# The value pass of a two-layer decoder: 25 pairs of value chunks by Strassen's scheme

## The chip, the cores and the metric

The kernel runs on one core of a Trainium2 chip. The metric is the device time of one execution in microseconds (us); the kernel before has a median of 1827.03 us over three runs (1826.66 to 1827.59). In the rows of a profile the engines are PE (TensorE, matrix products; PEld is its load of the stationary operand), DVE (VectorE), ACT (ScalarE), POOL (GpSimd) and SP, whose queue issues the loads.

## The reference, cut to what matters

Two layers transform x (256 tokens of 1024 numbers). Each has a token mixer and then a channel mixer in which every token picks 128 of 16384 experts (8 heads of 16) and adds up their value rows:

```python
        u = u_tab[eid]
        act = jax.nn.gelu(jnp.einsum('nhkd,nd->nhk', u, xb).astype(jnp.float32), approximate=False)
        coef = (gw * act).astype(x.dtype)
        return jnp.einsum('nhk,nhkd->nd', coef, v_tab[eid])
...
        x = layer_norm(DN_ALPHA * x + y, ln2_g[i], ln2_b[i])
```

The kernel doesn't gather. It computes `u_tab @ x` for all 16384 experts, multiplies by gates that are zero for experts not picked, and multiplies the resulting 16384 x 256 matrix of coefficients with the whole value table: `y = coef^T @ v_tab`, with 16384 rows of 1024 values read from memory once per layer. That last product is the value pass. Everything is fp32.

## The kernel before

**Three products for one.** The fast fp32 product of the PE keeps fewer bits than fp32. Each operand is therefore split in two: the high part H is the operand cast (on ACT, L100 for values, L236 for coefficients), the low part L is the operand minus H (on DVE, L115 and L237, or partly on POOL). `mm3` (L172) then issues three matmuls into one PSUM bank: H·H, H·L and L·H (L174 to L176). A value of `pool_cols` says how many columns of a low part POOL computes; in the value pass it is 0, so all of it lies on DVE.

**The value pass** (`peer_layer`, L1143 on) runs over 128 chunks of 128 experts. Chunk i has a coefficient tile of 128 experts x 256 tokens (`lo` holds chunks 0 to 63, `hi` the others) and a value tile of 128 experts x 1024 columns. The output is cut into two token tiles `tt` and two halves `k` of 512 columns, four PSUM banks `y[tt][k]` in which all chunks accumulate. A chunk is thus four products of 128 x 128 by 128 x 512, of three matmuls each: 12 matmuls.

**What is issued when.** There is no scheduler: each engine works through its instructions in the order in which the loop emits them, and waits at an instruction whose input or buffer isn't ready. Step i of the loop first calls `next` (L140), which through `pump` (L80) casts and subtracts the values of chunk i+2; then `coef(i + 2)` splits the coefficients of chunk i+2; then come the 12 matmuls of chunk i. There are three buffers of split values (`HL_BUFS`), so the cast of chunk i+2 waits until the PE has finished chunk i-1, whose buffer it takes. The loads come in on SP's queue into five buffers (`RAW_BUFS`), counted by `n_flight`; a chunk's buffer is given back when it has been split, and the next load is issued then.

**The end of the pass.** The last 3 chunks of layer 0 and the last 6 of layer 1 (`kept`) are held back, and their products are issued bank by bank, so that `norm` (L268) can begin on a bank that is complete: it adds it to ALPHA times x on DVE (L286) and goes on to the layer norm. In layer 1 three of the six have buffers of their own (`eH`, `eL`). Layer 0 also loads and splits, between its value chunks, the inputs for the next layer's attention memory: four `memT` parts (subtracted on POOL) and four `wkv` chunks (cast on ACT, subtracted on DVE), at chunks 68, 74, ... 110.

**Banks.** PSUM has eight banks of 512 columns; the pass uses four.

Of the kernel before, what the change touches and what calls it, by code (L numbers as in the profile page):

```python
# [7 lines left out]
F32 = mybir.dt.float32  # L8
F32R = mybir.dt.float32r
# [4 lines left out]
ALU = mybir.AluOpType  # L14
# [4 lines left out]
P = 128  # L19
D = 1024  # L20
T = 256
DT = 8
ALPHA = 4.0 ** 0.25
EPS = 1e-5
GSCALE = 32768.0
N0 = 64
# [21 lines left out]
class Trunk:  # L48
    def __init__(self, ctx, tc, A, out):
        self.ctx, self.tc, self.nc, self.A, self.out = ctx, tc, tc.nc, A, out  # L50
        pool = lambda name, bufs=1, **k: ctx.enter_context(tc.tile_pool(name=name, bufs=bufs, **k))
        self.const = pool("const")
        self.raw = pool("raw", RAW_BUFS)
        self.hl = pool("hl", HL_BUFS)
        self.small = pool("small", 2)
        self.ps = pool("ps", 8, space=PSUM)
        self.items = []
        self.flip = False
        self.sides = []
        self.n_load = self.n_split = self.n_got = self.n_flight = 0  # L60
        self.kept = {}
        self.loaded, self.split = {}, {}

    def bank(self):
# [15 lines left out]
    def pump(self, upto):  # L80
        nc = self.nc
        upto = min(upto, len(self.items))
        while self.n_split < upto:
            i = self.n_split
            self.load(i + 1)
            ap, n, dest, keep, cuts = self.items[i]
            r = self.loaded.pop(i)
            self.n_split += 1
            if keep is not None:
                self.kept[keep] = r  # L90
                continue
            if type(dest) is int:
                h, l = self.extra[dest]
            elif dest is None:
                h = self.hl.tile([P, D], F32R, name="wH")[:, :n]
                l = self.hl.tile([P, D], F32R, name="wL")[:, :n]
            else:
                h, l = dest()
            for c in cuts:
                (nc.vector.tensor_copy if self.cast_dve else nc.scalar.copy)(h[:, c], r[:, c])  # L100
            k = n if getattr(dest, "pool", False) else min(n, self.pool_cols)
            if len(cuts) > 1:
                for c in cuts:
                    e = (nc.vector, nc.gpsimd)[c.start > 0]
                    e.tensor_sub(l[:, c], r[:, c], h[:, c].bitcast(F32))
                k = n
            elif k and self.chained:
                nc.vector.tensor_sub(l[:, k:], r[:, k:], h[:, k:].bitcast(F32))  # L108
                k += 2
                nc.gpsimd.tensor_sub(l[:, :k], r[:, :k], h[:, :k].bitcast(F32))  # L110
                k = n
            elif k:
                nc.gpsimd.tensor_sub(l[:, :k], r[:, :k], h[:, :k].bitcast(F32))  # L113
            if k < n:
                rest = lambda l=l, r=r, h=h, k=k: nc.vector.tensor_sub(l[:, k:], r[:, k:], h[:, k:].bitcast(F32))  # L115
# [151 lines left out]

    def norm(self, y, last, early, fill=False):  # L268
        nc, x = self.nc, self.x
        fine = early or last  # L270
        while "b" not in self.kept:
            self.pump(self.n_split + 1)
        g, b = self.kept["g"], self.kept["b"]
# [4 lines left out]
        Q = 256  # L278

        def add(tt, k):  # L280
            if fine and tt and k:
                q0, n = 1 + k, 1
            else:
                q0, n = 2 * k, 2
            xs = x[:, tt, q0 * Q:(q0 + n) * Q]
            nc.vector.scalar_tensor_tensor(xs, xs, ALPHA, y[tt][k][:, :n * Q], op0=ALU.mult, op1=ALU.add)  # L286
            return tt, q0, n

        def half(tt, q0, n):
# [68 lines left out]
        if fill:  # L358
            yield
            part = add(1, 0)  # L360
# [666 lines left out]
    def peer_layer(self, layer):  # L1027
        nc, tc, A = self.nc, self.tc, self.A
        with ExitStack() as ctx:
# [110 lines left out]
            self.pool_cols, self.chained = 0, False  # L1140
            kept = HL_BUFS + (EXTRA if layer else 0)

            def coef(i):  # L1143
                src = lo[:, i, :] if i < N0 else hi[:, i - N0, :]
# [7 lines left out]
            gl = cp.tile([P, T], F32, name="gl", bufs=1)  # L1152
            nc.scalar.activation(gl, g, AF.Gelu)
            nc.vector.tensor_mul(hi[:, nj - 1, :], hi[:, nj - 1, :], gl)
            y = [[self.bank() for _ in range(2)] for _ in range(2)]
            late = []

            def products(tt, c0, n, part):
                t = slice(tt * P, (tt + 1) * P)
                k, o = divmod(c0, 512)  # L1160
                for i_, (h, l), (cH, cL) in part:
                    self.mm3(y[tt][k][:, o:o + n], cH[:, t], cL[:, t], h[:, c0:c0 + n], l[:, c0:c0 + n],
                             i_ == 0, i_ == P - 1)
            for i in range(P):
                if i + 2 > P - 1:
                    self.pool_cols = 512
                late.append((i, self.next(min(HL_BUFS, P - i)), cs.pop(0)))
                if i + 2 == N0:
# [45 lines left out]
    def plan(self):  # L1214
# [24 lines left out]
        def tail(layer):  # L1239
            for i, dt in enumerate(ORDER[layer]):  # L1240
                self.add(A["w_out"][layer, dt], D, i - 2 if 0 <= i - 2 < EXTRAS[layer] else None)
            norm("ln1", layer)
            for g in range(2):
                for dt in range(DT):
                    self.add(A["w_q"][layer, g, dt], D)
            for i in range(P):
                self.add(A["u"][layer, i], D)
            for i in range(P):
                e = i - P + HL_BUFS + EXTRA
                self.add(A["v"][layer, i], D, e if layer and 0 <= e < EXTRA else None)  # L1250
                k = (i - N0 - 4) // 6
                if layer == 0 and i > N0 and (i - N0 - 4) % 6 == 0 and 0 <= k < 8:
# [110 lines left out]
```

## Time and profile before

| | |
|---|---|
| median of 3 runs | 1827.03 us (1826.66 to 1827.59) |
| the profiled execution | 1825.44 us, its span 1823.7 us |
| PE busy | 1804.1 us, 99% of the span |
| DVE busy | 1307.6 us, 72% |
| ACT busy | 940.7 us, 52% |
| POOL busy | 429.2 us, 24% |
| value pass of layer 0, of layer 1 | 348.17 us from 576.70, 347.92 us from 1467.88 |

The span goes from the first to the last instruction on the core; the time of an execution lies 1.7 us above it. A matmul's record is longer than the time it adds to a stream of matmuls, since they are pipelined: what one adds is read from the starts of its neighbours. The same holds, less strongly, for DVE and ACT.

### The profile page before, as it was taken

The page shows a single profiled execution, that of the slowest core. Times are in us where ns is not written, and L with a number is a line of the kernel's source. Part 1 is how long each engine was busy: PE and PEld are TensorE (multiplying, and loading weights), DVE is VectorE, ACT ScalarE, POOL GpSimd, SP SyncE. Part 2 cuts the span into 40 slices and gives each one's busy share as a digit, 9 for nine tenths or more (in the row PEclk, how much of TensorE's full clock was granted, in tenths as well). Part 3 has the DMA queues.
Part 4 walks back from the last instruction along what each step waited for, and adds up shares of the span by engine and source line. Part 5 has one row for each costly group of instructions (what it writes and reads, how often), then busy time and mean ns, then how long its engine had stood idle before and what let it go on. Part 6 is the DMA issues. An engine that isn't in the chain of part 4 may idle for free.

```text
span 1823.7 us, 33361 instructions
## 1 busy us (share of the span) xinstructions
PE 1804.1 (99%) x12810; PEld 1666.1 (91%) x12810; DVE 1307.6 (72%) x2669; ACT 940.7 (52%) x1614; POOL 429.2 (24%) x324
## 2 busy tenths in 40 slices
PE   8999999999999999999999999999999999999998
PEld 8999999999999888888898899999999988888886
DVE  6684779499998555566668758686999965555556
ACT  6554555455544544555557354554555455444553
POOL 2015762433331000000001368325333300000000
PEclk9999999999999999999999999999999999999999
DMA  7556566655555666667645356666555556666664
GB/s 246 200 160 199 168 202 186 194 167 163 162 162 170 192 194 195 194 214 228 206 171 183 117 176 176 196 196 185 163 163 162 163 181 193 193 195 194 191 194 137
DMA packets 95552, 334.21 MB, mean 183 GB/s; under 512 B 10652, under 2 KB 13728, under 8 KB 95136
## 3 DMA queue, kind: packets, MB, share of 16 engines
q1 hardware_dynamic: 93752, 328.93, 59.2%
q10 hardware_dynamic: 1640, 3.15, 0.5%
q8 instruction: 100, 1.64, 0.4%
q14 instruction: 60, 0.49, 0.1%
HBM read 330.98 MB, written 1.05 MB: 182 GB/s over the span
## 4 chain that ended last, share of the span: by engine, by line
PE 73%; issue 17%; POOL 7%; DVE 2%; ACT 1%; DMA 0%; POOLq 0%; SPq 0%; DVEq 0%; ACTq 0%
PE bank L176 23%; PE bank L174 23%; PE bank L175 23%; POOL wL L110 7%; PE bank L240 2%; ACT wH L100 0%; DVE eL L115 0%; PE bank L333 0%; DVE eH L100 0%; POOL wL L113 0%; PE bank L233 0%; DMA cp<-in_rg_par_dram 0%; DMA raw<-in_w0kg_dram 0%; DVE x L286 0%; DVE wL L115 0%
## 5 line engine op out<-in xcount | busy, mean ns | idle before, releaser
L100 ACT CAST wH<-raw 128x1024 fp32r<-128x1024 f32 (+2 forms) x605 | 626.7, 1037 | 755.3 <-PE bank L176 321.5
L115 DVE TENSOR_TENSOR wL<-raw,wH 128x1024 fp32r<-128x1024 f32 (+3 forms) x413 | 465.6, 1130 | 434.5 <-ACT wH L100 433.9
L174 PE MATMUL bank<-xHL,wH 128*128 128x256 f32 x2536 | 715.2, 282 | 4.8 <-ACT wH L100 4.8
L176 PE MATMUL bank<-xHL,wL 128*128 128x256 f32 x2536 | 702.6, 277 | 0.5 <-DVE wL L115 0.5
L175 PE MATMUL bank<-xHL,wH 128*128 128x256 f32 x2536 | 702.4, 277 | 0.0
L174 PEld LDWEIGHTS bank<-xHL,wH 128*128 128x128 f32 x2536 | 477.4, 188 | 4.8 <-ACT wH L100 4.8
L176 PEld LDWEIGHTS bank<-xHL,wL 128*128 128x128 f32 x2536 | 477.2, 188 | 1.1 <-DVE wL L115 0.7
L175 PEld LDWEIGHTS bank<-xHL,wH 128*128 128x128 f32 x2536 | 477.9, 188 | 0.0
L175 PE MATMUL bank<-wL,cH 128*128 128x512 f32 x1015 | 394.3, 388 | 0.0
L174 PE MATMUL bank<-wH,cH 128*128 128x512 f32 x1015 | 394.3, 388 | 0.0
L176 PE MATMUL bank<-wH,cL 128*128 128x512 f32 x1015 | 394.3, 388 | 0.0
L113 POOL TENSOR_TENSOR wL<-raw,wH 128x1024 fp32r<-128x1024 f32 (+1 forms) x121 | 255.3, 2112 | 210.0 <-ACT wH L100 208.2
L174 PEld LDWEIGHTS bank<-wH,cH 128*128 128x128 f32 x1015 | 190.5, 188 | 39.6
L176 PEld LDWEIGHTS bank<-wH,cL 128*128 128x128 f32 x1015 | 190.5, 188 | 39.3
L175 PEld LDWEIGHTS bank<-wL,cH 128*128 128x128 f32 x1015 | 190.5, 188 | 39.0
L110 POOL TENSOR_TENSOR wL<-raw,wH 128x386 fp32r<-128x386 f32 x126 | 129.5, 1028 | 280.1 <-DVE wL L108 280.1
L322 POOL TENSOR_TENSOR x<-x,raw 128x256 f32<-128x256 f32 x6 | 4.9, 822 | 550.1 <-ACT x L319 550.1
L989 DVE TENSOR_TENSOR oh<-iota,i12T 128x1024 f16<-128x1024 f16 x128 | 130.4, 1019 | 0.0
L108 DVE TENSOR_TENSOR wL<-raw,wH 128x640 fp32r<-128x640 f32 x126 | 104.0, 825 | 7.5
L992 DVE TENSOR_TENSOR oh<-oh,gT 128x1024 f16<-128x1024 f16 x128 | 90.0, 703 | 4.4
L1122 PE MATMUL bank<-oh 128*128 128x128 f16 x1024 | 80.6, 219 | 1.1 <-DVE oh L992 1.1
L1122 PEld LDWEIGHTS <-oh 128*128 128x128 f16 x1024 | 58.6, 97 | 6.0 <-DVE oh L992 1.5
(289 smaller groups left out, 1552.2 us busy)
## 6 DMA issues: line engine op xcount, KB each, us to landing
raw<-in_u_dram SPq DMA_DIRECT2D x256, 512.0 KB, 3.6
raw<-in_v_dram SPq DMA_DIRECT2D x256, 512.0 KB, 4.2
raw<-in_w_q_dram SPq DMA_DIRECT2D x32, 512.0 KB, 4.3
raw<-in_w_out_dram SPq DMA_DIRECT2D x16, 512.0 KB, 4.3
raw<-in_w0qx_dram SPq DMA_DIRECT2D x8, 512.0 KB, 5.1
raw<-in_wkv_dram SPq DMA_DIRECT2D x8, 512.0 KB, 4.6
raw<-in_w0v_dram SPq DMA_DIRECT2D x8, 384.0 KB, 5.7
raw<-in_w0o_dram SPq DMA_DIRECT2D x8, 384.0 KB, 3.2
```

Of the source, the lines that this page charges most:

```text
L100: (nc.vector.tensor_copy if self.cast_dve else nc.scalar.copy)(h[:, c], r[:, c])
L108: nc.vector.tensor_sub(l[:, k:], r[:, k:], h[:, k:].bitcast(F32))
L110: nc.gpsimd.tensor_sub(l[:, :k], r[:, :k], h[:, :k].bitcast(F32))
L113: nc.gpsimd.tensor_sub(l[:, :k], r[:, :k], h[:, :k].bitcast(F32))
L115: rest = lambda l=l, r=r, h=h, k=k: nc.vector.tensor_sub(l[:, k:], r[:, k:], h[:, k:].bitcast(F32))
L174: mm(out, sH, mH, start=start, stop=False, skip_group_check=True)
L175: mm(out, sH, mL, start=False, stop=False, skip_group_check=True)
L176: mm(out, sL, mH, start=False, stop=stop, skip_group_check=True)
L240: self.nc.tensor.matmul(out, lhsT, rhs, start=start, stop=stop, skip_group_check=True)
L989: nc.vector.tensor_tensor(flat(oh[:, 1:3]), self.iota2.unsqueeze(1).to_broadcast([P, 4, P, 2]), pairs(self.i12T[:, j]), op=ALU.is_equal)
L992: nc.vector.tensor_tensor(flat(oh[:, 0:2]), two.rearrange("p z (q e t) -> p z q e t", q=2, t=2), pairs(self.gT[:, j]), op=ALU.mult)
L1122: nc.tensor.matmul(wp[:, qs], oh[:, 2, q // 2, :, q % 2], oh[:, z, q // 2, :, q % 2], start=z == 0, stop=z == 1, skip_group_check=True)
```

## The change

In each layer chunks 8k+2 and 8k+3 form a pair, for k = 1 to 13 (in layer 0 without k = 10): 12 and 13 pairs. Call the pair's coefficient blocks ta, ua (first chunk; tokens 0-127 and 128-255) and tb, ub, and its value halves a0, a1 and b0, b1. Instead of eight products the pair gets seven, by Winograd's form of Strassen's scheme:

- m1 += ta·a0, y[0][0] += tb·b0, y[0][1] += s3·b1, y[1][0] += ub·t3
- m5 += s0·t0, m7 += s1·t1, m6 += s2·t2
- sums of coefficients (128 wide): s1 = ta - ua, s2 = ub - s1, s3 = tb - s2, s0 = ua + ub
- sums of values (512 wide): t0 = a1 - a0, t1 = b1 - a1, t2 = t1 + a0, t3 = b0 - t2

m1, m5, m7 and m6 are four more PSUM banks that accumulate over all pairs of a layer. The sums are computed on DVE into blocks of `lo` or `hi` that are used up, and split like any operand (cast on ACT, subtraction on DVE) into parts of `xHL`, which isn't needed during the pass. `paired(i)` is called in each step behind `coef`, and deals this work out over the steps: the s in step 8k-1, t0 and t1 in step 8k, t2 and t3 in step 8k+1, the splits in steps 8k+4 to 8k+8. The PE issues one product in step 8k+2 (m1) and two in step 8k+3; the other four are `owed`: m5 stands at the end of step 8k+7, m7 and m6 at the end of the next pair's first step, ub·t3 at the end of its second. The layer's last pair has them in its own steps 8k+7 and 8k+8.

Further: of a pair's first chunk only the half a0 is split, since a1 occurs only in sums. The two raw buffers of a pair are given back in step 8k+1, after t3. In steps 113 to 120, behind the last pair (chunks 106 and 107) and its owed products, the four extra banks are added into x, one DVE instruction a step; x gets its factor ALPHA there, and the layer's last norm adds with a factor of 1. The `lo` tiles of both layers are given up at step 74 instead of 62, and layer 0's eight extra items move to chunks 80, 82, 84, 86 (`memT`) and 113, 116, 119, 122 (`wkv`).

```diff
+PAIRS = [[1, 2, 3, 4, 5, 6, 7, 8, 9, 11, 12, 13], list(range(1, 14))]
+CLOSE = 76
+MEM1 = (80, 82, 84, 86, 113, 116, 119, 122)
...
+            z = self.twin.get(i)
+            if z is not None:
+                if z == 0:
+                    self.pair = [r, self.loaded[min(q for q in self.twin if q > i)]]
+                n = min(n, 512 * (z + 1))
+                cuts = [slice(0, n)]
...
-            self.n_flight -= getattr(dest, "stage", None) is None
+            self.n_flight -= getattr(dest, "stage", None) is None and z is None
...
+        alpha = 1.0 if last or fill else ALPHA
...
+            def paired(i):
+                k, j = divmod(i, 8)
+                if j == 0 and k - 1 in PAIRS[layer]:
+                    cast_sums(k - 1, 3, 1, 0)
+                if j == 7 and k + 1 in PAIRS[layer]:
+                    (ta, ua), (tb, ub) = part(i + 3), part(i + 4)
+                    _, s = sums32(k + 1)
+                    nc.vector.tensor_sub(s[:, 1], ta, ua)
+                    nc.vector.tensor_sub(s[:, 2], ub, s[:, 1])
+                    nc.vector.tensor_sub(s[:, 3], tb, s[:, 2])
+                    nc.vector.tensor_add(s[:, 0], ua, ub)
+                if k in PAIRS[layer]:
...
+                    if j == 0:
+                        nc.vector.tensor_sub(t[0], a1, a0)
+                        nc.vector.tensor_sub(t[1], b1, a1)
+                    elif j == 1:
+                        nc.vector.tensor_add(t[2], t[1], a0)
+                        nc.vector.tensor_sub(t[3], b0, t[2])
+                        self.n_flight -= 2
+                        self.load(len(self.items))
+                    elif j == 4:
+                        nc.scalar.copy(sh[:, 0:3], s[:, 0:3])
+                        nc.scalar.copy(sh[:, 3], part(i - 1)[1])
+                        nc.vector.tensor_sub(sl[:, 0:3], s[:, 0:3], plain(sh[:, 0:3]))
+                        nc.vector.tensor_sub(sl[:, 3], part(i - 1)[1], plain(sh[:, 3]))
+                        cast_sums(k, 0, 2, 0)
+                    elif j == 5:
+                        split_sums(k, 0, 2, 0)
+                        cast_sums(k, 2, 1, 2)
+                    elif j == 6:
+                        split_sums(k, 2, 1, 2)
+                if j == 0 and k - 1 in PAIRS[layer]:
+                    split_sums(k - 1, 3, 1, 0)
...
+                n = i - done
+                if n == 1:
+                    nc.scalar.copy(q, m1)
+                    onto(0, 0, m1)
+                elif n == 2:
+                    nc.vector.tensor_add(q, q, m6)
...
+                elif n == 8:
+                    onto(1, 1, m5, 1.0)
...
+            owed = {}
+            for k, n in zip(PAIRS[layer], PAIRS[layer][1:] + [None]):
+                e = 8 * k + 7
+                for m, at in enumerate((e, 8 * n + 2, 8 * n + 2, 8 * n + 3) if n else (e, e, e, e + 1)):
+                    owed.setdefault(at, []).append((k, m))
...
+                paired(i)
                 if i + 1 > P - kept:
                     continue
-                for tt in range(2):
-                    for k in range(2):
-                        products(tt, 512 * k, 512, late)
+                if i in first or i - 1 in first:
+                    (_, (h, l), (cH, cL)), = late
+                    if i in first:
+                        mixed(m1, h[:, :512], l[:, :512], (cH[:, :P], cL[:, :P]), first[i])
+                    else:
+                        mixed(y[0][0], h[:, :512], l[:, :512], (cH[:, :P], cL[:, :P]))
+                        mixed(y[0][1], h[:, 512:], l[:, 512:], (cH[:, P:], cL[:, P:]))
+                else:
+                    for tt in range(2):
+                        for k in range(2):
+                            products(tt, 512 * k, 512, late)
+                for k, m in owed.get(i, ()):
+                    if m == 3:
+                        mixed(y[1][0], th[:, 0], tl[:, 0], (sh[:, 3], sl[:, 3]))
+                    else:
+                        mixed((m5, m7, m6)[m], th[:, m], tl[:, m], (sh[:, m], sl[:, m]), k)
```

`cast_sums` and `split_sums` are one ACT copy and one DVE subtraction over 512 columns for each sum. `coef` splits only ta for a pair's first chunk, and tb and s3 for its second.

More of the change, by code (lines that the diff above doesn't have):

```diff
@@ L61, in __init__ @@
         self.kept = {}
+        self.twin, self.pair = {}, [None, None]
         self.loaded, self.split = {}, {}
@@ L1141, in peer_layer @@
             kept = HL_BUFS + (EXTRA if layer else 0)
-            def coef(i):
-                src = lo[:, i, :] if i < N0 else hi[:, i - N0, :]
+            block = lambda i: lo[:, i, :] if i < N0 else hi[:, i - N0, :]
+            part = lambda i: [block(i)[:, :P], block(i)[:, P:]]
+            first = {8 * k + 2: k for k in PAIRS[layer]}
+            done = 8 * PAIRS[layer][-1] + 8
+            gl = cp.tile([P, T], F32, name="gl", bufs=1)
+            th, tl = self.xHL[:, 0:3, :], self.xHL[:, 3:6, :]
@@ new lines, in peer_layer, with sums32, split_sums @@
+            sh, sl = (self.xHL[:, f, :].rearrange("p (f t) -> p f t", f=4) for f in (6, 7))
+            plain = lambda a: a.bitcast(F32)
+            def sums32(k):
+                old = hi if k > 8 else lo
+                flat = lambda b: old[:, b:b + 2, :].rearrange("p a b -> p (a b)")
+                return [flat(b) for b in (0, 2, 4, 6)], flat(8).rearrange("p (f t) -> p f t", f=4)
+            def split_sums(k, f, n, s):
+                old = hi if k > 8 else lo
+                t = old[:, 2 * f:2 * (f + n), :].rearrange("p (f a) b -> p f (a b)", f=n)
+                nc.vector.tensor_sub(tl[:, s:s + n], t, plain(th[:, s:s + n]))
@@ new lines, in cast_sums, with onto @@
+            def cast_sums(k, f, n, s):
+                old = hi if k > 8 else lo
+                t = old[:, 2 * f:2 * (f + n), :].rearrange("p (f a) b -> p f (a b)", f=n)
+                nc.scalar.copy(th[:, s:s + n], t)
+            def paired(i):
[10 more added lines that the diff above has]
+                if k in PAIRS[layer]:
+                    t, s = sums32(k)
+                    if j < 2:
+                        (a0, a1), (b0, b1) = [[r[:, :512], r[:, 512:]] for r in self.pair]
+                    if j == 0:
[19 more added lines that the diff above has]
+                    split_sums(k - 1, 3, 1, 0)
+                q = hi[:, 0:2, :].rearrange("p a b -> p (a b)")
+                def onto(t, h, src, scale=ALPHA):
+                    xs = self.x[:, t, 512 * h:512 * h + 512]
+                    nc.vector.scalar_tensor_tensor(xs, xs, scale, src, op0=ALU.mult, op1=ALU.add)
+                n = i - done
[4 more added lines that the diff above has]
+                    nc.vector.tensor_add(q, q, m6)
+                elif n == 3:
+                    onto(0, 1, q)
+                elif n == 4:
+                    onto(0, 1, m5, 1.0)
+                elif n == 5:
+                    nc.vector.tensor_add(q, q, m7)
+                elif n == 6:
+                    onto(1, 0, q)
+                elif n == 7:
+                    onto(1, 1, q)
+                elif n == 8:
+                    onto(1, 1, m5, 1.0)
@@ L1155, in peer_layer @@
             y = [[self.bank() for _ in range(2)] for _ in range(2)]
+            m1, m5, m7, m6 = [self.bank() for _ in range(4)]
             late = []
@@ L1167, in peer_layer @@
                 late.append((i, self.next(min(HL_BUFS, P - i)), cs.pop(0)))
[L1168 removed]
+                if i + 2 == CLOSE:
                     right.close()
@@ L1249, in tail @@
                 e = i - P + HL_BUFS + EXTRA
+                if i % 8 in (2, 3) and i // 8 in PAIRS[layer]:
+                    self.twin[len(self.items)] = i % 8 - 2
                 self.add(A["v"][layer, i], D, e if layer and 0 <= e < EXTRA else None)
-                k = (i - N0 - 4) // 6
-                if layer == 0 and i > N0 and (i - N0 - 4) % 6 == 0 and 0 <= k < 8:
+                if layer == 0 and i in MEM1:
+                    k = MEM1.index(i)
                     if k < 4:
```

20 lines of the change are left out of this document (17 added, 3 removed).

## Prediction

> **What bounds the kernel now.** The page first: who is busy, and which engine the chain that ended last runs over.
>
> ```profile
> PE 1804.1 (99%) x12810; PEld 1666.1 (91%) x12810; DVE 1307.6 (72%) x2669; ACT 940.7 (52%) x1614; POOL 429.2 (24%) x324
> ...
> PE 73%; issue 17%; POOL 7%; DVE 2%; ACT 1%; DMA 0%; POOLq 0%; SPq 0%; DVEq 0%; ACTq 0%
> ```
>
> PE is busy all the time and carries the chain; but busy records overlap, so I look at the two value passes alone, by windows (length, then busy time and count of PE, PEld, DVE, ACT, POOL, the granted clock, the DMA engines' share, GB/s).
>
> ```profile
> 576.70:924.87 348.17, 348.17 (x1538) 288.28 (x1537) 211.23 (x267) 179.62 (x264) 7.87 (x6) 1.00 0.66 201
> 1467.88:1815.80 347.92, 347.41 (x1548) 288.01 (x1547) 203.40 (x267) 172.42 (x255) 3.28 (x4) 1.00 0.64 189
> ```
>
> PE never rests in the first and 0.5 us in the second, at full clock; DVE is 61% busy (211.23/348.17). 348.17 us over 128 chunks of 12 matmuls is 2.72 us a chunk and 0.2267 us a matmul. One chunk's step in the timeline (start, duration, engine, line) shows the order behind it:
>
> ```profile
> 599.83 0.39 PE L174 MATMUL bank<-wH,cH 128*128 128x512 f32 x1
> ...
> 600.96 0.39 PE L176 MATMUL bank<-wH,cL 128*128 128x512 f32 x1
> ...
> 601.39 1.05 ACT L100 CAST wH<-raw 128x1024 fp32r<-128x1024 f32 x1 [1.36 <-PE bank L176]
> ...
> 602.34 0.40 ACT L236 CAST cH<-wglo 128x256 fp32r<-128x256 f32 x1
> ...
> 602.47 1.22 DVE L115 TENSOR_TENSOR wL<-raw,wH 128x1024 fp32r<-128x1024 f32 x1 [1.16 <-ACT wH L100]
> ...
> 602.55 0.39 PE L174 MATMUL bank<-wH,cH 128*128 128x512 f32 x1
> ...
> 603.62 0.42 DVE L237 TENSOR_TENSOR cL<-wglo,cH 128x256 fp32r<-128x256 f32 x1
> ```
>
> The last matmul of a chunk ends at 601.35 (600.96 + 0.39); 0.04 later the cast starts that takes over the buffer, and the low part follows, done 2.34 us after the PE let go (603.69 - 601.35). It isn't needed until two more chunks have run, 5.44 us: DVE may be some 3 us late before PE feels it. DVE's idle 1.16 us a step is the room in which the change must fit.
>
> **The gain.** A pair needs 7 products of 3 matmuls instead of 8: 25 pairs x 3 = 75 matmuls fewer, x 0.2267 = 17.0 us. Every other matmul keeps its shape (128x128 by 512), and the order only moves whole products. New is that the owed ones stream their moving operand from `xHL`; the u products before the pass do that with 256 columns, in starts of 0.80/7 = 0.114 us, twice which is the same 0.227:
>
> ```profile
> 575.78 0.28 PE L175 MATMUL bank<-xHL,wH 128*128 128x256 f32 x1
> ...
> 576.58 0.28 PE L176 MATMUL bank<-xHL,wL 128*128 128x256 f32 x1
> ```
>
> So the price of one stays. Eight chunks now last 31 x 3 x 0.2267 = 21.08 us on PE, not 21.76; per step: 2.72, with 2.04 in steps 8k+2 and 8k+3 (nine matmuls each, owed ones included) and 3.40 in step 8k+7 (fifteen).
>
> I weigh the price of a matmul against a rule: the Trainium skill ("TensorE: Matmul & The Clock Gate", Back-to-back issue gap) gives about 131 ns for one of N=512 in a sustained stream, and by it the gain would be an estimated 9.8 us. This trace has 227 ns in a stream without a gap, and that decides.
>
> **What DVE gets.** What an instruction adds is the distance of starts. A run of DVE work near the end of the second pass gives it, and shows a tight spot:
>
> ```profile
> 1791.68 1.22 DVE L115 TENSOR_TENSOR wL<-raw,wH 128x1024 fp32r<-128x1024 f32 x1 [1.16 <-ACT wH L100]
> ...
> 1793.16 1.22 DVE L115 TENSOR_TENSOR eL<-raw,eH 128x1024 fp32r<-128x1024 f32 x1
> 1794.30 0.42 DVE L237 TENSOR_TENSOR cL<-wghi,cH 128x256 fp32r<-128x256 f32 x1
> 1794.63 1.22 DVE L115 TENSOR_TENSOR eL<-raw,eH 128x1024 fp32r<-128x1024 f32 x1
> ...
> 1800.59 1.22 DVE L115 TENSOR_TENSOR wL<-raw,wH 128x1024 fp32r<-128x1024 f32 x1
> ```
>
> 1024 columns add 1.14 us (1793.16 to 1794.30), 256 add 0.33 (to 1794.63). 512 columns add 0.60 (932.48 to 933.08 below), and where an instruction reads what the last one wrote, it waits for its end and 0.04 more (931.02 to 931.81, one of 0.75):
>
> ```profile
> 931.02 0.75 DVE L307 SCALAR_TENSOR_TENSOR x<-x,mv,raw 128x512 f32<-128x512 f32 x1
> 931.81 0.75 DVE L312 SCALAR_TENSOR_TENSOR x<-x,rs,raw 128x512 f32<-128x512 f32 x1
> 932.48 0.69 DVE L115 TENSOR_TENSOR wL<-raw,wH 128x512 fp32r<-128x512 f32 x1
> 933.08 0.75 DVE L237 TENSOR_TENSOR xHL<-bank,xHL 128x256 fp32r<-128x256 f32 x2
> ```
>
> For 128 and 384 columns the line through 256 and 1024 gives 0.20 and 0.47; dependent 128 and 512 cost 0.33 and 0.73 (whole durations, 0.29 and 0.69, plus 0.04), from
>
> ```profile
> L115 DVE TENSOR_TENSOR wL<-raw,wH 128x1024 fp32r<-128x1024 f32 x316 | 386.5, 1225 | 312.5 <-ACT wH L100 312.0
> ...
> L286 DVE SCALAR_TENSOR_TENSOR x<-x,bank 128x512 f32<-128x512 f32 x13 | 8.8, 679 | 10.3 <-PE bank L176 10.3
> ...
> L829 DVE TENSOR_TENSOR th<-th,rr 128x512 f32<-128x512 f32 x3 | 2.1, 689 | 0.9 <-ACT th L826 0.9
> ...
> L717 DVE TENSOR_TENSOR hn<-hn,so 128x384 f32<-128x384 f32 x4 | 2.0, 552 | 0.0
> ...
> L965 DVE TENSOR_TENSOR gw<-gw,gsum 128x128 f32<-128x128 f32 x4 | 1.2, 293 | 0.1
> ```
>
> Per group of eight chunks, by step (PE's length of the step in brackets), the ordinary work being 1.14 + 0.33 = 1.47:
> - 8k+7 (3.40): 1.47, and the s: 3 x 0.33 + 0.20 = 1.19; 2.66
> - 8k (2.72): half a value and ta, 0.60 + 0.20; t0 and t1, 1.20; one split, 0.60; 2.60
> - 8k+1 (2.72): 1.14 + 2 x 0.20; t2 and t3, 2 x 0.73; 3.00
> - 8k+2, 8k+3 (2.04 each): 1.47 each
> - 8k+4 (2.72): 1.47 + 0.47 + 0.20 = 2.14
> - 8k+5 (2.72): 1.47 + 1.14 = 2.61
> - 8k+6 (2.72): 1.47 + 0.60 = 2.07
>
> In all 18.0 of 21.08 us: DVE goes from 54% to 85% of PE's time, and only step 8k+1 is longer than PE's own, by 0.28. Its 0.28 is caught up in the step after, within the 3 us (two short steps leave 2 x 2.04 - 2.34 = 1.7). So in the steady run I count nothing; the cover is this slack, and without it each pair costs what it lacks.
>
> ACT: a group adds casts of 384, 128 and 4 x 512 columns and drops 512; at 1.05 us for 1024 that is about 2 us beside 8 x 1.45 (1.05 + 0.40) = 11.6, of 21.08. Hidden. In step 8k+4 the sums' casts run into the next step by about 0.6 us, which the same slack takes.
>
> **Two places without cover.** (1) The first pair of a layer: nothing is owed yet, so steps 10 and 11 last 0.68 and 1.36. Count from T, the end of chunk 9 on PE. DVE's step 9 begins at T - 2.72 + 1.12 = T - 1.60 and ends 3.00 later, T + 1.40; the values of chunk 12 are then split by T + 2.62 (1.22). PE wants them at T + 2.04 + 0.23 = T + 2.27: a stall of 0.35, and the coefficients behind them (0.42, wanted by the third matmul 0.23 later) add 0.2. With one or two waits between ACT and DVE in that step, up to 1.0. I take 0.8 a layer, 1.6. (2) The end of layer 1. The run above splits seven chunks without a pause, from 1791.68 to 1800.59 + 1.22 = 1801.81. Chunk 122, the first held back, starts here:
>
> ```profile
> 1798.57 0.39 PE L174 MATMUL bank<-eH,cH 128*128 128x512 f32 x1
> ```
>
> Chunk 127, the sixth, is wanted at 1798.57 + 5 x 0.68 + 0.23 = 1802.20: 0.39 to spare. Steps 119 and 120 now put two additions into x into this run, 512 columns each, 0.60 to 0.68 (L286): 1.3 - 0.39 = 0.9 of stall. The six earlier ones have 1.2 us of room a step.
>
> **Moved loads.** No transfer is added. A pair's two raw buffers stay until t3, T + 1.40 with T the end of step 8k+1; the loads of chunks 8k+7 and 8k+8 are queued on SP behind that.
>
> ```profile
> raw<-in_v_dram SPq DMA_DIRECT2D x256, 512.0 KB, 4.2
> ```
>
> The first lands at about T + 5.6, the cast wants it at T + 2.04 + 2.04 + 2.72 = T + 6.8; the second is wanted 2.7 later. A load that leaves later can't gain anything; it costs something from a landing time of 5.4 us on, and PE feels it 3 us later still; at a DMA share of 0.66 I count nothing. Four `wkv` splits (1.14) fall among the additions in steps 113 to 122 of layer 0: three steps hold 3 x (1.47 + 0.65) + 1.14 = 7.5 of 8.16; nothing. The norms keep their instructions, and their waits:
>
> ```profile
> PE bank L174 <- DVE x L286: 0.5, 1, 0.5
> ```
>
> **Sum.** -17.0 + 1.6 + 0.9 = -14.5 us. The profiled execution took 1825.44, 1.6 below the median; on the median, 1827.03 - 14.5 = 1812.5.
>
> **Rivals.** (a) DVE loses its overlap. If each of the 30 DVE instructions of a group waited for the end of the one before and 0.04 more, as the pair at 931 does, the group would cost its full durations: 7 x 1.225 + 0.69 for values, 6 x 0.42 + 3 x 0.29 for coefficients, 4 x 0.29 + 5 x 0.69 + 0.55 + 0.29 + 1.225 for sums, 20.0, and 1.2 of hand-over: 21.2 of 21.08. DVE then sets the pace, 25 x 0.15 = 4, and the stalls at (1) and (2) about double, 2: 1818.5. For it: most new instructions wait for ACT or for DVE itself; against it: ordinary splits wait for ACT too and keep 1.14. The Trainium skill ("VectorE: DVE Perf Modes", The DRAIN you can't avoid) says that the next Vector instruction doesn't start before the pipeline has emptied, unless it is one that isn't held; the first half would speak for (a). The rows at 1794.30 and 1794.63, 0.33 apart with a record of 0.42, disagree for neighbours that don't depend on each other.
>
> (b) Slower than before. If DVE's group grows beyond PE's old 21.76 us, the pass is paced by DVE and longer than before: this needs 21.8/18.0, every DVE instruction 21% dearer, say by operands that lie in `lo`, raw and `xHL` at once while PE reads `xHL`. At 25% it is 22.5, 25 x 0.74 = 18.5 slower: 1845. No row of this size (POOL idle) shows such a stretch.
>
> (c) No change that can be measured: a gain of up to 3.7 us is within 0.2%, about what a measurement of this kernel can tell. It takes a DVE group of 21.5 to 21.8 us, 20 to 21% above my sum, between (a) and (b).
>
> **Chances.** The forecast 0.74, (a) 0.13, (b) 0.08, (c) 0.05. Faster is the forecast and (a), 0.87; same 0.05; slower 0.08. Range: from no stall at all, 1810.0, less half a microsecond for the scatter of runs, to (a) and a little more: 1809.5 to 1821.
>
> **What will show it.** The two passes should last about 341 us each (348.17 - 12 x 0.68 + 0.8; 347.92 - 13 x 0.68 + 1.7), PE idle only around chunk 12 and, in layer 1, chunks 125 to 127; DVE busy near 80% there; matmuls still 0.227 apart with `xHL` as moving operand. PE waits of 0.2 us or more in every pair on DVE's low parts mean (a) or (b), and on ACT's casts that loads or casts are late. The prediction is wrong if the sums' DVE records are longer than 0.69 and 0.29, or if DVE rests in steps 8k and 8k+1, waiting on ACT or a raw chunk with later splits queued behind.

## The result and the profile after

| | before | after |
|---|---|---|
| median of 4 runs | 1826.85 us (1825.53 to 1827.59) | 1813.74 us (1813.66 to 1814.23) |
| the profiled execution, its span | 1825.44, 1823.7 us | 1813.66, 1811.9 us |
| value pass of layer 0 | 348.18 us | 341.88 us |
| value pass of layer 1 | 349.36 us | 343.47 us |

The ratio after/before is 0.993, with a 95% interval of 0.9912 to 0.9947: faster by 13.1 us on the medians, 11.8 between the two profiled executions (the one of before was 1.4 below its median). The forecast was 1812.5.

A pass is taken here from the start of its first matmul to the start of the PE's next work (in layer 1, where no matmul follows, to 0.11 us after the start of its last one); the prediction's window for layer 1 began 1.2 us into the pass. The first lines of the page of after answer to those shown of before: busy time by engine, and the engines of the chain that ended last.

```profile
PE 1791.1 (99%) x12735; PEld 1652.1 (91%) x12735; DVE 1451.5 (80%) x3035; ACT 993.4 (55%) x1766; POOL 430.9 (24%) x324
...
PE 71%; issue 17%; POOL 7%; DVE 3%; ACT 1%; DMA 0%; POOLq 0%; SPq 0%; DVEq 0%; ACTq 0%
```

75 matmuls fewer (12810 to 12735), 366 DVE instructions more, and the PE is still the engine that is never at rest. By windows (length, then busy time and count of PE, PEld, DVE, ACT, POOL, the clock, the DMA share, GB/s), the passes of after and one group of eight chunks with its pair:

```profile
577.07:918.95 341.88, 341.60 (x1502) 281.48 (x1501) 282.19 (x443) 204.86 (x337) 8.81 (x6) 1.00 0.62 204
1460.79:1804.26 343.47, 342.28 (x1517) 281.64 (x1515) 282.22 (x458) 200.44 (x335) 3.27 (x4) 1.00 0.59 192
649.35:670.53 21.18, 21.18 (x95) 17.46 (x93) 18.11 (x31) 12.93 (x23) 0.00 (x0) 1.00 0.59 201
```

DVE is busy 282.19 of 341.88 us (83%) and 18.11 us in a group of 21.18; PE has 0.28 us without a record in layer 0 and 1.19 in layer 1. The passes are shorter by 6.30 and 5.89 us, 12.19 together. Outside them little changed: the first pass begins 0.37 us later (577.07 against 576.70), and from the first pass to the second it takes 541.84 us, against 541.83 before. So the account has to close inside the passes, where the prediction had -14.5.

The waits of the PE inside the two passes of after (in total, times, longest), first layer 0, then layer 1:

```profile
PE bank L185 <- DVE wL L125: 0.3, 1, 0.3
```

```profile
PE bank L185 <- DVE wL L125: 0.7, 2, 0.4
PE bank L184 <- DVE x L297: 0.5, 1, 0.5
```

The last row is the norm's wait that was there before. The others stand at the two places named in the prediction. The timeline of after around chunk 12 (start, duration, engine, line, operation):

```profile
606.33 0.39 PE L184 MATMUL bank<-wH,cH 128*128 128x512 f32 x1
607.00 0.50 PE L185 MATMUL bank<-wL,cH 128*128 128x512 f32 x1 [0.28 <-DVE wL L125]
607.34 0.49 PE L186 MATMUL bank<-wH,cL 128*128 128x512 f32 x1
607.67 0.40 PE L184 MATMUL bank<-wH,cH 128*128 128x512 f32 x1
```

The distances are 0.67, 0.34 and 0.33 in place of 0.227: 0.44 for the wait, and 0.11 and 0.10 because the two matmuls behind it come more slowly. The place costs 0.65 us, not the 0.28 of the list of waits. At the end of layer 1, chunks 126 and 127:

```profile
1788.81 0.45 PE L185 MATMUL bank<-wL,cH 128*128 128x512 f32 x1
1789.10 0.50 PE L186 MATMUL bank<-wH,cL 128*128 128x512 f32 x1
1789.43 0.40 PE L184 MATMUL bank<-wH,cH 128*128 128x512 f32 x1
1790.23 0.49 PE L185 MATMUL bank<-wL,cH 128*128 128x512 f32 x1 [0.40 <-DVE wL L125]
1790.56 0.50 PE L186 MATMUL bank<-wH,cL 128*128 128x512 f32 x1
1790.90 0.39 PE L184 MATMUL bank<-eH,cH 128*128 128x512 f32 x1
```

Over the 0.227 of each these are 0.06, 0.10, 0.57, 0.10 and 0.11: 0.94 us.

With these stalls the passes should have lasted 348.18 - 12 x 0.68 + 0.65 = 340.67 and 349.36 - 13 x 0.68 + 0.65 + 0.94 = 342.11 us. They lasted 341.88 and 343.47: 1.21 and 1.36 more, 0.10 for every pair, with no wait of the PE to show for it. That remainder, 2.57 us, and the cause of the stall at chunk 12 are what the experiments are about.

### The profile page after: what moved, and what is told of

It reads as the page before. It is cut to its first block, busy times and chain, and to the rows that moved or that the text cites. A ratio compares the mean times of both kernels' runs of the same rounds, so it can differ in the third digit from the quotient of the medians.

```text
span 1811.9 us, 33750 instructions
## 1 busy us (share of the span) xinstructions
PE 1791.1 (99%) x12735; PEld 1652.1 (91%) x12735; DVE 1451.5 (80%) x3035; ACT 993.4 (55%) x1766; POOL 430.9 (24%) x324
## 4 chain that ended last, share of the span: by engine, by line
PE 71%; issue 17%; POOL 7%; DVE 3%; ACT 1%; DMA 0%; POOLq 0%; SPq 0%; DVEq 0%; ACTq 0%
PE bank L186 23%; PE bank L185 23%; PE bank L184 23%; POOL wL L120 7%; PE bank L250 2%; ACT wH L110 1%; DVE eL L125 0%; DVE wL L125 0%; PE bank L344 0%; DVE eH L110 0%; POOL wL L123 0%; PE bank L243 0%; DMA raw<-in_w0kg_dram 0%; DMA cp<-in_rg_par_dram 0%; DVE x L297 0%
## 5 line engine op out<-in xcount | busy, mean ns | idle before, releaser
L110 ACT CAST wH<-raw 128x1024 fp32r<-128x1024 f32 (+3 forms) x605 | 615.9, 1019 | 689.6 <-PE bank L186 222.1
L125 DVE TENSOR_TENSOR wL<-raw,wH 128x1024 fp32r<-128x1024 f32 (+3 forms) x413 | 451.7, 1096 | 276.1 <-ACT wH L110 274.4
L185 PE MATMUL bank<-wL,cH 128*128 128x512 f32 x890 | 346.4, 389 | 1.0 <-DVE wL L125 1.0
L186 PE MATMUL bank<-wH,cL 128*128 128x512 f32 x890 | 346.7, 390 | 0.0
L184 PE MATMUL bank<-wH,cH 128*128 128x512 f32 x890 | 345.9, 389 | 0.0
L185 PEld LDWEIGHTS bank<-wL,cH 128*128 128x128 f32 x890 | 167.0, 188 | 37.7 <-DVE wL L125 2.5
L186 PEld LDWEIGHTS bank<-wH,cL 128*128 128x128 f32 x890 | 167.0, 188 | 35.3
L184 PEld LDWEIGHTS bank<-wH,cH 128*128 128x128 f32 x890 | 167.1, 188 | 35.0
```

The source lines that it names most:

```text
L125: rest = lambda l=l, r=r, h=h, c=slice(k, n): nc.vector.tensor_sub(l[:, c], r[:, c], h[:, c].bitcast(F32))
L184: mm(out, sH, mH, start=start, stop=False, skip_group_check=True)
L185: mm(out, sH, mL, start=False, stop=False, skip_group_check=True)
L186: mm(out, sL, mH, start=False, stop=stop, skip_group_check=True)
```

## The experiments

**The same kernel again**, for the scatter.

> The changed kernel once more, on the same chip as the three that follow, so that differences of 1 us can be read: 1813.7 us, within 0.5.

1813.94 us (1813.1 to 1814.18), passes 341.88 and 343.43. Between these two traces a pass repeats to within 0.04 us, so differences of 0.1 us in a pass can be read, though the medians scatter by half a microsecond.

**The last two sums of a layer's first pair one step later**, where DVE has room.

```diff
-                    if j < 2:
+                    late_t = j - (k == PAIRS[layer][0])
+                    if j < 3:
...
-                    elif j == 1:
+                    elif late_t == 1:
                         nc.vector.tensor_add(t[2], t[1], a0)
```

> Only the first pair of each layer: t2 and t3 stand one step later (step 10 instead of 9), so that DVE splits chunk 12 about 1.4 us earlier. Theory (PE sets the pace, the two short steps without owed products are a hole): the wait at chunk 12, about 0.65 us in each layer's trace, falls to 0.1, and the time by 1.0 to 1.3 us. Rival (the DVE work as a whole is what lags, and chunk 12 is only where it surfaces first): the wait moves to a later chunk and the time stays.

1813.93 us (1813.01 to 1814.29), passes 341.87 and 343.47: nothing gained. The wait at chunk 12 in the timeline of this kernel:

```profile
606.89 0.39 PE L184 MATMUL bank<-wH,cH 128*128 128x512 f32 x1
607.46 0.50 PE L185 MATMUL bank<-wL,cH 128*128 128x512 f32 x1 [0.18 <-DVE wL L125]
```

The expected microsecond isn't there: the wait is shorter by 0.10 us only, though DVE is free when the cast is done. What is late can be seen on ACT and DVE, first in the kernel after, then in this one:

```profile
604.53 1.05 ACT L110 CAST wH<-raw 128x1024 fp32r<-128x1024 f32 x1 [1.31 <-issue]
...
605.73 1.22 DVE L125 TENSOR_TENSOR wL<-raw,wH 128x1024 fp32r<-128x1024 f32 x1
```

```profile
605.09 1.05 ACT L110 CAST wH<-raw 128x1024 fp32r<-128x1024 f32 x1 [1.31 <-issue]
...
606.18 1.22 DVE L125 TENSOR_TENSOR wL<-raw,wH 128x1024 fp32r<-128x1024 f32 x1 [1.13 <-ACT wH L110]
```

In the kernel after DVE begins the split 1.20 us after ACT began the cast, here 1.09: DVE had been 0.11 us late. The cast itself starts only when the PE has given the buffer back, and cast, hand-over and split take 1.09 + 1.22 = 2.31 us from there. The two short steps, with no owed work yet, last 0.68 + 1.36 = 2.04 us together and leave 2.04 + 0.23 = 2.27 until the PE wants the low part; the hand-overs from PE to ACT and from DVE to PE come on top of the 2.31. The chain from release to split is longer than the two steps, whatever DVE does.

The 0.10 us don't show in the length of the pass because they are lost again one chunk later. By the starts of the matmuls this trace is 0.10 us ahead of the kernel after at chunk 12, and 0.01 us from the end of chunk 13 on. With t2 and t3 moved ahead of it on DVE, the split of chunk 13 comes late in its turn:

```profile
608.98 1.22 DVE L125 TENSOR_TENSOR wL<-raw,wH 128x1024 fp32r<-128x1024 f32 x1
610.12 0.42 DVE L247 TENSOR_TENSOR cL<-wglo,cH 128x256 fp32r<-128x256 f32 x1
```

The low parts of its coefficients are done at 610.54 (608.76 in the kernel after, whose pass began 0.56 us earlier). The third matmul of chunk 13, the first to use them, starts at 610.66, and the next follows only at 610.92, 0.26 us later. Something like the rival named before the run has happened, on a small scale: what chunk 12 gains, chunk 13 loses.

**The additions at the end two to a step**, in steps 113 to 116 instead of 113 to 120.

```diff
-                n = i - done
-                if n == 1:
+                for n in (2 * (i - done) - 1, 2 * (i - done)):
+                    if n == 1:
```

> The eight additions into x stand two to a step in steps 113 to 116 instead of one to a step in 113 to 120. Theory: DVE is done with them before the run of seven splits at layer 1's end, the PE's waits there (0.9 us) go, and the time falls by 0.9 us; in layer 0, where two extra chunks are split in the same steps, nothing happens (DVE is late by at most 1.3 us of the 3 it may be). Rival (the end of layer 1 is bound by ACT or by the loads): no change; or the layer 0 pile-up makes it slower by up to 1 us.

1812.98 us (1811.99 to 1814.29), ratio to before 0.9928 (0.9912 to 0.9945). The pass of layer 0 stays, that of layer 1 is 0.98 us shorter (343.47 to 342.49), and one of its two waits of the PE for DVE is gone:

```profile
1460.65:1803.14 342.49, 341.69 (x1517) 281.82 (x1515) 282.31 (x458) 200.43 (x335) 3.29 (x4) 1.00 0.58 192
```

```profile
PE bank L184 <- DVE x L297: 0.5, 1, 0.5
PE bank L185 <- DVE wL L125: 0.3, 1, 0.3
```

So the stall at the end came from the two additions within the run of splits.

**Both edits together.**

> Both edits together. Theory: the two gains add, 1.9 to 2.2 us below the changed kernel, 1811.6 us; the value passes then last 341.3 and 342.0 us, with no wait of PE on DVE left but the 0.5 us before the last products. Rival: less than 1 us in all.

1813.05 us (1812.91 to 1813.46), ratio 0.9928 (0.9911 to 0.9945), passes 341.89 and 342.45: what the second edit gives, and nothing from the first.

**The sums' work on DVE and ACT left out.** `paired` only gives the raw buffers back.

> The sums are left out (no s, no t, no casts or splits of them); the owed products read whatever xHL holds, and everything else stays, so the output is not the reference's. It prices all the DVE and ACT work of the pairs at once. Theory (that work is hidden apart from chunk 12 in each layer): the time falls by 1.2 to 1.5 us, the length of a group of eight chunks with a pair stays at 21.18 us. If the 0.1 us by which a group is longer than 31 x 3 matmuls (21.08) comes from the sums' traffic or their signals, the group falls to 21.08 and the time by another 2.3. Rival (a) (DVE lags in every pair): more than 4 us.

1813.66 us (1813.03 to 1813.91). The pass of layer 0 by windows:

```profile
576.87:918.60 341.73, 341.59 (x1502) 281.46 (x1501) 205.45 (x287) 173.35 (x277) 8.78 (x6) 1.00 0.66 204
```

DVE has 77 and 82 us less to do in a pass, ACT 32 and 34, and the passes are shorter by 0.15 and 0.14 (layer 1 takes 343.33), where 1.2 to 1.5 us in all were expected. By the starts, the 0.15 of layer 0 lies at chunk 12 alone: apart from that, the new work on DVE and ACT is hidden. The remainder of 0.10 us a pair isn't theirs, and chunk 12 still costs about half a microsecond here: its distances in this trace are 0.53, 0.34 and 0.33. With no sums on DVE, what stands before the split is the cast, and before the cast the PE:

```profile
604.28 1.05 ACT L110 CAST wH<-raw 128x1024 fp32r<-128x1024 f32 x1 [1.27 <-PE bank L186]
```

**The owed products with operands of the chunk at hand**, none from `xHL`. The sums' work stays.

```diff
-                        mixed((m5, m7, m6)[m], th[:, m], tl[:, m], (sh[:, m], sl[:, m]), k)
+                    (_, (h, l), (cH, cL)), = late
+                    mixed(y[1][0] if m == 3 else (m5, m7, m6)[m], h[:, :512], l[:, :512],
+                          (cH[:, :P], cL[:, :P]), None if m == 3 else k)
```

> The sums are computed and split as before, but the owed products take their operands from the buffers of the current chunk (wH, wL, cH, cL) instead of xHL, so the output is not the reference's. Same matmuls, same DVE and ACT work. If the 0.1 us a group is the price of operands in xHL or of the signals between DVE and PE on them, groups last 21.08 us and the time falls by 2.3 us; if it comes from the DVE and ACT traffic, nothing changes.

1811.07 us (1810.41 to 1813.08), and the remainder is gone:

```profile
576.56:917.25 340.69, 340.40 (x1502) 281.46 (x1501) 283.52 (x443) 204.69 (x337) 8.80 (x6) 1.00 0.63 205
1459.09:1801.22 342.13, 340.94 (x1517) 281.62 (x1515) 283.50 (x458) 200.51 (x335) 3.28 (x4) 1.00 0.59 192
```

340.69 and 342.13, where 340.67 and 342.11 were worked out above. So the excess goes with the operands from `xHL`. The next three kernels ask which operand.

**Only the moving operand from `xHL`, or only the stationary one.** One line each in place of the one above.

```diff
+                    mixed(..., th[:, f], tl[:, f], (cH[:, :P], cL[:, :P]), ...)
```

> The owed products stream their moving operand from xHL as in the changed kernel, but load the current chunk's coefficients (cH, cL) as the stationary one; sums still computed, output not the reference's. Read from the trace's passes (341.88 and 343.45 us in the changed kernel, 340.69 and 342.13 with both operands from the chunk). If the moving operand in xHL costs the extra 0.1 us a group: 341.9 and 343.4. If the stationary operand does, or both operands lying in one tile: 340.7 and 342.1.

```diff
+                    mixed(..., h[:, :512], l[:, :512], (sh[:, m], sl[:, m]), ...)
```

> The other way round: the stationary operand comes from xHL (sh, sl), the moving one from the current chunk's wH and wL; output not the reference's. If the stationary operand's place costs the 0.1 us a group: 341.9 and 343.4. If it costs only where both lie in xHL, or if the moving operand's place does it: 340.7 and 342.1.

1815.6 and 1811.21 us (one run each). The pass of layer 0 with the moving operand from `xHL`, then with the stationary one:

```profile
577.06:919.43 342.37, 342.08 (x1502) 281.44 (x1501) 282.58 (x443) 204.72 (x337) 8.81 (x6) 1.00 0.62 204
```

```profile
576.45:917.48 341.03, 340.74 (x1502) 281.53 (x1501) 282.77 (x443) 205.02 (x337) 8.80 (x6) 1.00 0.62 205
```

Over the 340.69 of the kernel without `xHL`, the moving operand from there costs 1.68 us a pass, the stationary one 0.34; layer 1 says the same (343.92 and 342.49, against 342.13). Both from `xHL` (the kernel after) cost 1.19, less than the moving one alone: the two don't add up.

**The moving operand from the next chunk's split values**, to tell `xHL` from the mere fact that the product leaves the chunk at hand.

```diff
+                    hn, ln = self.split[self.n_got]
+                    mixed(..., hn[:, :512], ln[:, :512], (cH[:, :P], cL[:, :P]), ...)
```

> The owed products stream their moving operand from the split values of the next chunk (already in place, another buffer of the same pool as wH), with the current chunk's coefficients as the stationary operand; sums computed, output not the reference's. With the moving operand from xHL and the same stationary one the passes were 342.37 and 343.92 us, with both from the current chunk 340.69 and 342.13. If a change of the moving operand's buffer in the middle of a step costs the time: about 342 and 343.6. If it is xHL as the source: 340.7 and 342.1.

1811.58 us (one run), passes 340.73 and 342.12: no excess. The starts of the same products tell it directly, m7 and m6 of one pair and the ordinary product behind them, first in the kernel with `xHL` as moving operand alone, then in this one:

```profile
645.94 0.39 PE L184 MATMUL bank<-xHL,cH 128*128 128x512 f32 x1
...
646.64 0.39 PE L184 MATMUL bank<-xHL,cH 128*128 128x512 f32 x1
...
647.34 0.39 PE L184 MATMUL bank<-wH,cH 128*128 128x512 f32 x1
```

```profile
645.75 0.39 PE L184 MATMUL bank<-wH,cH 128*128 128x512 f32 x1
...
646.43 0.39 PE L184 MATMUL bank<-wH,cH 128*128 128x512 f32 x1
...
647.11 0.39 PE L184 MATMUL bank<-wH,cH 128*128 128x512 f32 x1
```

With the chunk's own coefficients as stationary operand, a product of three matmuls takes 0.70 us from `xHL` and 0.68 from the buffers of the value chunks.

That isn't a price of every read of `xHL`, as the kernel after itself shows. There both operands of an owed product lie in `xHL`, and the products that begin with m7 and m6 of the same pair start at

```profile
645.89 0.39 PE L184 MATMUL bank<-xHL 128*128 128x512 f32 x1
...
646.59 0.39 PE L184 MATMUL bank<-xHL 128*128 128x512 f32 x1
...
647.27 0.39 PE L184 MATMUL bank<-wH,cH 128*128 128x512 f32 x1
...
647.96 0.40 PE L184 MATMUL bank<-wH,cH 128*128 128x512 f32 x1
...
648.65 0.39 PE L184 MATMUL bank<-xHL 128*128 128x512 f32 x1
```

The first owed product takes 0.70 us, the one right behind it 0.68, and the two ordinary ones that follow 0.69 each. Over layer 0 (612 to 900 us), an owed product right behind another takes 0.679 us on average (13 of them), the other 35 take 0.694, the first and the second ordinary product behind a run of owed ones 0.692 and 0.688, and those after them 0.680. So more than half of the excess lies in products that don't read `xHL` at all. And the kernel before has products of 0.70 us where no operand comes from `xHL`: at the end of layer 1, where the last six chunks have their coefficients in buffers of the pool `ends`. In these rows three products on `wH` are followed by three on `eH`, which lies in `ends` too:

```profile
1800.63 0.40 PE L174 MATMUL bank<-wH,cH 128*128 128x512 f32 x1
...
1802.73 0.40 PE L174 MATMUL bank<-eH,cH 128*128 128x512 f32 x1
...
1804.78 0.40 PE L174 MATMUL bank<-wH,cH 128*128 128x512 f32 x1
```

The three on `wH` take 2.10 us, the three on `eH` 2.05. What the longer products share is a certain pair of places for the two operands (`xHL` with the chunk's coefficients, `wH` with those in `ends`), or a change of places just before. That this is the cause wasn't tested.

**The places within `xHL` exchanged** (value sums in its last blocks, coefficient sums in its first), on top of the edit at the end.

```diff
-            th, tl = self.xHL[:, 0:3, :], self.xHL[:, 3:6, :]
+            th, tl = self.xHL[:, 2:5, :], self.xHL[:, 5:8, :]
```

> The kernel with two additions to a step, and within xHL the places are exchanged: the split coefficient sums take the first quarter, the split value sums the rest, 4 KB further up in each partition. If the 0.1 us a group depends on where in the memory the moving operand lies, the passes change by more than 0.2 us from 341.9 and 342.5 (in either direction). If it goes with the owed products whatever their place inside xHL: 341.9 and 342.5, and 1813.0 us.

1812.56 us (1812.21 to 1813.08), ratio 0.9925 (0.9908 to 0.9941); passes 341.93 and 342.49, those of the edit at the end alone. Which block of `xHL` is read doesn't matter. With the edit at the end alone (1812.98), this is the best version with all the sums and products of the change: about 1 us below the kernel after, 13 to 14 below the one before.

**DVE loaded further.** One more subtraction a step in 88 steps of each layer, 256 or 512 columns wide.

```diff
+                spent = lo if 16 <= i < 72 else hi if 80 <= i < 112 else None
+                if spent is not None:
+                    extra = spent[:, 10:12, :].rearrange("p a b -> p (a b)")[:, :256]
+                    nc.vector.tensor_sub(extra, extra, extra)
```

> One more DVE subtraction of 256 columns (0.33 us) in each step 16 to 71 and 80 to 111 of both layers, on a block that is used up: 2.64 us a group, 20.7 us of DVE work beside 21.18 of PE. Theory (DVE has 85% of PE's time to do, and may be some 2 us late): no change, within 0.7 us. Rival (a) (DVE without overlap, already at 21.2 us a group): 24.9 us a group and 21 groups, about 75 us slower.

1815.09 us (1814.37 to 1815.65), but the passes are those of the kernel after, 341.88 and 343.46, with 27 us more of DVE work in each:

```profile
577.68:919.56 341.88, 341.60 (x1502) 281.50 (x1501) 309.46 (x531) 204.90 (x337) 8.80 (x6) 1.00 0.63 204
```

DVE at 91% of the pass, and at 20.61 of the 21.18 us of a group, still costs the PE nothing. The profiled execution is 2.0 us above that of the kernel after (the median 1.35), and all of it lies outside the passes, where the code is the same: 0.61 us ahead of the first, 0.53 between them, 0.86 behind the last product. What it is wasn't found.

> The same with 512 columns (0.60 us): 4.8 us a group, 22.8 us of DVE work, more than PE's 21.18. Theory: DVE now sets the pace in 21 groups with a pair, 21 x 1.65 = 35 us, less what the slack before and the lighter groups behind take up: 25 to 35 us slower than the changed kernel. If nothing happens, DVE's work per group is overestimated.

1835.72 us (one run). Now DVE sets the pace; the pass of layer 0 and one group by windows, and the PE's wait in that pass:

```profile
576.47:928.45 351.98, 344.96 (x1502) 280.73 (x1501) 330.17 (x531) 204.81 (x337) 9.84 (x6) 1.00 0.62 199
671.96:694.56 22.60, 21.61 (x94) 17.40 (x94) 22.50 (x39) 12.93 (x24) 0.00 (x0) 1.00 0.59 185
```

```profile
PE bank L185 <- DVE wL L125: 7.0, 9, 1.0
```

The passes are 10.10 and 11.19 us longer, and the time is up by 22 us where 25 to 35 were expected. A group lasts 22.60 us, of which DVE is busy 22.50; the sum by rows (18.0 + 8 x 0.60) gave 22.8, so that sum is too high, by 0.2 to 0.3, rather than too low. This is what the rivals (a) and (b) would have looked like: the PE waits for a low part up to 1 us at a time, nine times in the pass.

## Why the prediction was right, and where it was off

**The gain** of 75 matmuls stood on 0.2267 us each, and it is there: with the operands taken from the value buffers the passes are, to 0.02 us, those of before less 8.16 and 8.84 us plus the measured stalls. The 131 ns that the Trainium skill ("TensorE: Matmul & The Clock Gate", Back-to-back issue gap) gives for a matmul of N=512 in a sustained stream would have meant an estimated 9.8 us. The two passes lost 17.0 less the stalls and the excess, so the trace disagrees with it here.

**"So the price of one stays"** is the term that was mis-sized. It was argued from the u products, which read `xHL` as moving operand in 256 columns at 0.114. Those read it all the time; the owed products leave the value buffers for `xHL` and come back, 35 times in layer 0 and 38 in layer 1. This going to and fro was put at nothing and cost 2.57 us, 35 ns for each of the 73 runs of owed products: part of it in the owed products (0.231 us a matmul, unless one directly follows another), part in the two ordinary ones behind. (With only the moving operand from `xHL` it was 3.47 us in the two passes.) The prediction's own trace had a sign of it, the products of 0.70 us in the stretch from which place (2) was worked out. This is the whole of the miss and a little more: inside the passes -12.19 was measured and -14.5 expected, 2.31 apart, which is +2.57 for this and -0.26 for the stalls. That the time came nearer to the forecast than the passes did, 1.2 us above it, is chance: the medians differ by 13.1 us, the two profiled executions by 11.8.

**Place (1), chunk 12:** 0.65 us a layer against 0.8. The size was nearly right, the reason mostly not. The prediction's count had DVE as the late one, with the values split by T + 2.62; DVE was late by 0.11 us only. With the sums left out, 0.52 us remained. So most of it is that these two steps, 2.04 us together, are shorter than the chain from the release of a buffer over cast and split. The prediction had both numbers in hand, 2.34 us from the release to the end of the split and 2.27 until it is wanted, but held only DVE's own count against the 2.27. In later pairs the owed products lengthen the same steps to 2.04 each, and no wait is listed there.

**Place (2), the end of layer 1:** 0.94 against 0.9, for the reason given; moving the additions gave 0.98 back. The waits are at chunks 126 and 127.

**DVE's 18.0 us of a group** were measured as 18.11. The timeline of after has the spacings that the sum was made of: 128 columns, the second dependent on the first and the third not (0.32 and 0.21), and 512 columns, independent (0.60):

```profile
660.61 0.29 DVE L1189 TENSOR_TENSOR wglo<-wglo 128x128 f32<-128x128 f32 x1
660.93 0.29 DVE L1190 TENSOR_TENSOR wglo<-wglo 128x128 f32<-128x128 f32 x1
661.14 0.28 DVE L1191 TENSOR_TENSOR wglo<-wglo 128x128 f32<-128x128 f32 x1
...
662.15 0.69 DVE L1197 TENSOR_TENSOR wglo<-raw 128x512 f32<-128x512 f32 x1
662.75 0.68 DVE L1198 TENSOR_TENSOR wglo<-raw 128x512 f32<-128x512 f32 x1
663.35 0.69 DVE L1174 TENSOR_TENSOR xHL<-wglo,xHL 128x512 fp32r<-128x512 f32 x1
```

Neighbours of 512 columns start 0.60 apart with records of 0.69. So rival (a) falls: independent instructions overlap, and the first half of the rule of the Trainium skill ("VectorE: DVE Perf Modes", The DRAIN you can't avoid), by which the next would wait until the pipeline is empty, shows here only between instructions that depend on each other. (In the sum of rival (a), 5 x 0.69 should read 6 x 0.69: only so does it come to the 20.0 us and the 30 instructions named.) Rivals (b) and (c) needed a DVE group of 21.5 us or more. With 256 more columns a step a group has 20.61 us of DVE work, 2.5 more than in the kernel after, and the PE still sets the pace; with 512 more it has 22.50, and DVE does.

**ACT, loads, `wkv`:** costed at nothing, and nothing was seen. Without the sums' casts the passes are 0.15 us shorter at most; the loads land in 4.1 us (median of 256), where 5.4 would have begun to matter.

## What to carry to other kernels

Where PE is never at rest, count the matmuls that go, and then hold the length of the pass against that count: a remainder with no wait beside it lies in the price of the instructions, and it is found by changing one operand's place at a time, and then by the starts of single products: an average over the owed ones would have hidden that the second of two in a row costs nothing extra. By this, owed products that stand together should cost less than single ones; no run here tries it. When steps are made shorter, compare each run of short steps with the whole chain that hands a buffer round (release, cast, split, hand-overs), not with one engine's sum. The cost of a wait is the widening of the starts around it (0.65 us), not its entry in the list of waits (0.28).

## What was not expected of the hardware

Matmuls of the same shape don't all take the same time in a stream without a gap. Three of 128x512 take 0.680 us with the value buffers and the chunk's coefficients, `xHL` with the chunk's coefficients 0.700 (every one of 48 owed products in layer 0), `wH` with coefficients from `xHL` 0.687, both operands from `xHL` 0.694 where the place has just changed and 0.679 where it hasn't. Behind a run of owed products that read their moving operand from `xHL`, two ordinary products take 0.69, and the third 0.680 again. Which block of `xHL` holds the operand makes no difference. Nothing in these runs says why: the u products pair `xHL` with `wH`, 256 columns at a time, and start 0.114 us apart, half of the plain 0.227.

After a wait the PE's next matmuls come more slowly: 0.33 to 0.34 us to the next start for two of them, with records of 0.49 to 0.50 instead of 0.39, at a granted clock of 1.00. A short wait therefore costs about 0.2 us more than itself.
